# GpSimd's share of a feed-forward moved to VectorE, and one plain group in place of two, in a two-layer decoder trunk

## The chip, the cores and the metric

One core of one Trainium2 chip runs the whole program in one launch. The metric is the device time of one execution in microseconds; where several runs stand, the median is used. The engines are called as in the profile: PE (TensorE), PEld (its weight loads), DVE (VectorE), ACT (ScalarE), POOL (GpSimd), SP (the queue that issues the DMAs).

## The reference

The input is x, 1024 tokens of 1024 features in float32. Each of two layers does this (cut to what matters; d_ff is 2816):

```
h = rmsnorm(x);  proj = h @ w_in          # four token mixers read proj
y_a, y_b, y_c, y_d = latent attention, gated convolution, causal pooling, window attention
x = x + rmsnorm_per_group(y_a, y_b, y_c, y_d) @ w_o
h2 = rmsnorm(x)
gate, up = split(h2 @ w_gate_up)
x = x + (silu(gate) * up) @ w_down
```

A last rmsnorm follows. The change touches the feed-forward (the last three lines) and its neighbourhood.

## The kernel before

**Layout and exactness.** Features lie on the 128 partitions, tokens along the columns, in two token halves of 512 (`HT`). A float32 operand is split into two fp32r parts, hi and lo: ScalarE copies hi (L283, or L286 with a gain), VectorE makes lo as the difference (L284, L287). A product of two operands is then three TensorE instructions per 128-deep block, hi*hi, hi*lo and lo*hi (`mm3`, L272), each 128x128 by 128x512.

**The feed-forward by block products.** The activations are seen as a 2x2 matrix of blocks: even and odd feature tiles by the two token halves (B11, B21 of the one half, B12, B22 of the other; `hb` holds four tiles of each). The weights w_gate_up are handled in 22 groups `f` of 128 columns of d_ff; class `GateUp` loads a group's 2 x 512 KB (L1126). There are two ways to do a group:

- *plain*: `plain(f, u)` makes, for token half u, the gate from two block products and the up from two more, in PSUM banks taken from the rotation "wide". Both halves together make eight block products of four blocks each. `plain_gates`, `plain_silus`, `plain_acts` finish them.
- *seven products* (a Strassen-like form, the main loop over f from `NPL` to 21): it needs sums of weight blocks (`sums`, L1132 to L1134, and `sum4`, L1154, all on GpSimd) and sums of activation blocks N1, N2, T3, T4, which `combine(j)` makes on VectorE from both halves of feature tiles 2j and 2j+1. `gu_start` makes the first two products, on B11 and B21 only; the partial sums k1, k2, k5 are copied out of PSUM by ScalarE (`snap`, L1176) and added on VectorE (L1188, L1502, L1514).

`silu(g, r)` is ScalarE's Silu (L1311) followed by a product on GpSimd (L1312). `second` and `neg_mul` (L1305) make the activations. `combos(g)` (L1321, L1323) makes the sums of activation blocks that w_down's seven products need and writes them to DRAM. The sums of w_down's blocks are made meanwhile by the generator `dn_sums` (L157 to L164): per chunk a DMA in, four GpSimd sums of 128x256 (L161), a DMA out; 22 chunks a layer. The main loop steps it on with `next(sums, None)`.

With `NPL = 2` groups 0 and 1 are plain, so that TensorE has products to make as soon as one token half's residual is done (`out_last`, L1099), while VectorE still makes the other half's and the combinations.

**Storage.** 47 places of 4 KB per partition (`Slots`) serve weights and activations; PSUM has eight banks in four tags, mm (2), s (3), t (2), pv (1). `ps(tag)` takes the next bank of a tag, or of a rotation in `turns`.

**Order of the work.** The program order above is only a proposal. `order_engines` reads all instructions (`steps_of`), and `arrange` plays them through with a length for each (`length`) and writes the order of each engine's queue. Its rank is the program's own number plus a shift from the table `MOVES`, found by a search. Each engine then takes its queue strictly in that order. All of this runs on the host ahead of the launch.

Of the kernel before, what the change touches and what calls it, by code (L numbers as in the profile page):

```python
# [41 lines left out]
NPL = 2  # L42
# [69 lines left out]
def trunk_kernel(ctx: ExitStack, tc: tile.TileContext, ins, out):  # L112
# [37 lines left out]
    def dn_sums(l):  # L150

        n = HT // 2
        for c in range(0, NK // 2 * NG * P, n):
            cols = slice(c, c + n)
            i = F.pair()
            v = F.ap2(i).rearrange("p (b n) -> p b n", b=4)
            sp.dma_start(v, ins["w_dn"][l, :, :, cols].rearrange("b p n -> p b n"))  # L157
            yield
            b11, b12, b21, b22 = (v[:, k] for k in range(4))
            for k, (o, u) in enumerate(((b22, b21), (b21, b11), (b11, b22), (b12, b11))):  # L160
                pool.tensor_tensor(out=o, in0=o, in1=u, op=ALU.add)  # L161
# [225 lines left out]
    for l in range(L):  # L387
# [731 lines left out]
        class GateUp:  # L1119
# [8 lines left out]
            def sums(self):  # L1128
                w1, w2 = self.raw
                q = self.q = F.pair()  # L1130
                a11, a22, a21 = F.ap(w1), F.ap(w1 + 1), F.ap(w2 + 1)
                pool.tensor_tensor(out=F.ap(q + 1), in0=a21, in1=a22, op=ALU.add)  # L1132
                pool.tensor_tensor(out=F.ap(q), in0=a21, in1=a11, op=ALU.add)
                pool.tensor_tensor(out=a21, in0=F.ap(q + 1), in1=a11, op=ALU.add)  # L1134
# [17 lines left out]
            def sum4(self):  # L1152
                q4 = F.ap(self.raw[1])
                pool.tensor_tensor(out=q4, in0=q4, in1=F.ap(self.raw[1] + 1), op=ALU.add)  # L1154
# [24 lines left out]
        def gu_start(w, between=None):  # L1179

            w.pa, pd = ps("aa"), ps("ad")
# [5 lines left out]
            w.gate = tmp("tp")  # L1187
# [56 lines left out]
        for n in range(2):  # L1244
            R.free(kb_[1][n][1])
            R.free(va[2 + n][1])
        ma1 = norm_a(1)
        mix_values(*prev)
        for n in range(2):
            R.free(kb_[1][n][0])  # L1250
            R.free(va[n][1])
        ma0 = norm_a(0)
        out_some(len(parts))
# [3 lines left out]
        std = [GateUp(f) for f in range(2)]  # L1257
        std[0].split_plain()
# [4 lines left out]
        std[1].split_plain()  # L1263
# [4 lines left out]
        def plain(f, u):  # L1268

            w, b = std[f], ((B11, B21), (B12, B22))[u]  # L1270
            pg, pu = ps("wide"), ps("wide")
# [37 lines left out]
        def silu(g, r):  # L1309
            nonlocal last_silu  # L1310
            last_silu = act.activation(g, g, AF.Silu)  # L1311
            pool.tensor_tensor(out=g, in0=g, in1=r, op=ALU.mult)  # L1312
# [113 lines left out]
        w = GateUp(2)  # L1426
        plain(0, 0)
        combine(0)
        plain(1, 0)
        norm(0)  # L1430
        combine(1)
        plain_gates()
        plain(0, 1)
        norm(1)
        plain_silus()
        plain_gates()
        w.sums()
        combine(2)
        plain_acts()
        w.split1()  # L1440
        plain(1, 1)
        plain_silus()
        plain_gates()
        combine(3)
        w.split2()
        plain_acts()
# [3 lines left out]
        wn = GateUp(3)  # L1450
        w.split3()
        plain_silus()
        w.sum4()
        w.split4()
        plain_acts()
        for f in range(NPL, NFF):
            if wn:
                wn.sums()
            wnn = GateUp(f + 2) if f + 2 < NFF else None
            end = f == NFF - 1  # L1460
            gu_start(w, lambda: pending and second(*pending))
# [11 lines left out]
            if wn:  # L1473
# [5 lines left out]
            for i in w.s2:  # L1479
                R.free_pair(i)  # L1480
            k2 = snap(w.pa)
            if wn:
# [37 lines left out]
            neg_mul(F.ap(acts[f][0]), w.pa, gate)  # L1520
            if wn:
# [137 lines left out]
class Step:  # L1659
    __slots__ = ("ins", "eng", "rank", "before", "after", "tiles", "left", "ns", "tail", "ready", "sums", "bank", "onchip", "size", "start", "end", "table", "rows", "place")  # L1660

    def __init__(self, eng, rank):
# [4 lines left out]
        self.onchip = 0.0  # L1667
# [40 lines left out]
def length(eng, kind, i, ins, outs):  # L1708
    n = max(width(a) for a in ins + outs)
    ps = any(a.bass_ap.tensor.name.startswith("ps_") for a in ins)  # L1710
    if eng == "POOL":
        return 206 if kind == "InstMemset" else 1150 + 0.5 * n
# [19 lines left out]
def steps_of(tc):  # L1732
    steps, seen = [], {}
    table, runs = None, {"Silu": [], "Exp": []}
    for i in tc.nc.cur_bb.bb.instructions:
# [31 lines left out]
        else:  # L1767
            v.ns = length(eng, kind, i, ins, outs)
            if not any(a.bass_ap.tensor.name.startswith("ps_") for a in ins + outs):
                v.onchip = 0.7 if kind == "InstTensorScalarPtr" and len(ins) < 3 else 0.4  # L1770
# [39 lines left out]
def arrange(steps, rank=lambda v: v.rank):  # L1810
    queue, uses, freed, parked = {}, {}, {}, {}
# [21 lines left out]
    wire, pool_busy, last_fp32, table = 0.0, [], False, "Exp"  # L1833
# [5 lines left out]
    def takes(v, t):  # L1839
        for name in (x for x in v.tiles if x not in live):  # L1840
            tag = name.rsplit("_", 1)[0]
            if queue[tag][0] != name or not freed[tag] or freed[tag][0] + 40 > t:
# [3 lines left out]
    while any(now.values()) or any(later.values()):  # L1846
# [23 lines left out]
        for name in (x for x in v.tiles if x not in live):  # L1870
            tag = name.rsplit("_", 1)[0]
            if queue[tag][0] != name or not freed[tag]:
# [9 lines left out]
        for name in [x for x in v.tiles if x not in live]:  # L1882
            tag = name.rsplit("_", 1)[0]
            live.add(name)
            queue[tag].popleft()
            heapq.heappop(freed[tag])
# [17 lines left out]
        else:  # L1904
# [5 lines left out]
            if e == "DVE" and v.onchip:  # L1910
                ns += v.onchip * sum(max(0.0, min(b, t + ns) - max(a, t)) for a, b in pool_busy[-8:])
# [5 lines left out]
            if e == "POOL":  # L1917
                pool_busy.append((t, v.end))
# [6 lines left out]
        for name in v.tiles:  # L1925
            todo[name] -= 1
# [221 lines left out]
```

## Time and profile before

| | us |
|---|---|
| median of 3 runs | 2062.74 |
| lowest, highest | 2061.73, 2062.99 |
| the profiled execution, its own time | 2061.72 |
| its span, first to last instruction | 2059.9 |
| first layer: mixers, feed-forward entry, body, w_down | 0 to 380, to 520, to 840, to 1030 (about) |
| second layer: the same | 1030 to 1380, to 1520, to 1840, to 2060 (about) |

Some 1.8 us of the profiled execution lie outside the span. TensorE's granted clock is 0.998 of full speed over the span. Apart from small memsets GpSimd is at work from about 360 to 840 and from about 1400 to 1870 us. A row of the groups view reads: line, engine, operation, output and inputs with shapes, count | busy us, mean ns | idle time before it and what ended it. A row of the timeline reads: start, duration, engine, line, operation, count, and in brackets the idle time before it with what ended it. Matmul rows overlap (a row of 0.39 us starts every 0.23 us), so the busy share of PE is read as "no gap".

### The profile page before, as it was taken

The numbers are of one execution on the slowest core, as the hardware profiler recorded it, in microseconds if no ns is written. First come the engines' busy times: TensorE is split into PE (matmuls) and PEld (weight loads), VectorE is DVE, ScalarE is ACT, GpSimd is POOL, SyncE is SP. The second block draws the span as 40 slices with busy tenths as digits, with TensorE's granted clock in tenths as the row PEclk, the third lists the DMA queues.
The fourth block names the chain that finished last, engine by engine and source line by source line (L and its number), as shares of the span: only waits on it lengthen the run. The fifth ranks groups of instructions, "written<-read, shape, count | busy, mean of one in ns | idle before, by whom it ended". The sixth has DMA issues, their size and how long they took to land.

```text
span 2059.9 us, 26292 instructions
## 1 busy us (share of the span) xinstructions
PE 2033.0 (99%) x9418; PEld 1676.4 (81%) x9418; DVE 1553.8 (75%) x2430; ACT 979.5 (48%) x1722; POOL 596.9 (29%) x461
## 2 busy tenths in 40 slices
PE   8999999999999999999999999999999999999997
PEld 7887888878888888888888878878778888888887
DVE  7879988987776768655657898879877677686555
ACT  7447666653333334444443576666433333355332
POOL 0000000058776765100000000001787677640000
PEclk9999999999999999999999999999999999999999
DMA  5010222334444437866401102142444444498652
GB/s 181 34 58 24 79 88 86 138 121 168 170 156 167 166 138 257 313 221 204 152 33 44 47 21 91 64 144 81 160 168 163 153 166 153 145 333 278 197 177 86
DMA packets 148819, 289.76 MB, mean 141 GB/s; under 512 B 12608, under 2 KB 72000, under 8 KB 148688
## 3 DMA queue, kind: packets, MB, share of 16 engines
q1 hardware_dynamic: 148656, 288.03, 40.2%
q8 instruction: 74, 1.21, 0.2%
q14 instruction: 57, 0.47, 0.1%
q0 software_dynamic: 32, 0.04, 0.0%
HBM read 204.66 MB, written 83.36 MB: 140 GB/s over the span
## 4 chain that ended last, share of the span: by engine, by line
PE 89%; DVE 7%; DMA 1%; issue 1%; ACT 1%; POOL 1%; SPq 0%; DVEq 0%; ACTq 0%
PE ps_mm L272 35%; PE ps_s L272 26%; PE ps_t L272 10%; PE ps_pv L272 8%; DVE u L284 2%; PE ps_pv L962 2%; PE ps_t L950 1%; DVE u L287 1%; PE ps_s L896 1%; DVE u L324 1%; PE ps_t L336 1%; PE ps_s L898 1%; PE ps_s L897 1%; PE ps_pv L572 1%; DVE u L1099 1%
## 5 line engine op out<-in xcount | busy, mean ns | idle before, releaser
L272 PE MATMUL ps_mm<-u,u 128*128 128x512 f32 (+1 forms) x3394 | 848.8, 388 | 9.9 <-ACT u L286 7.1
L272 PEld LDWEIGHTS ps_mm<-u,u 128*128 128x128 f32 x3394 | 622.8, 188 | 136.2 <-ACT u L286 7.1
L272 PE MATMUL ps_s<-u,u 128*128 128x512 f32 x2648 | 649.4, 390 | 4.7 <-DVE u L284 3.6
L272 PEld LDWEIGHTS ps_s<-u,u 128*128 128x128 f32 x2648 | 496.8, 188 | 110.1 <-DVE u L284 4.4
L284 DVE TENSOR_TENSOR u<-u,u 128x1024 fp32r<-128x1024 f32 (+2 forms) x384 | 463.9, 1230 | 148.8 <-ACT u L283 129.3
L283 ACT CAST u<-u 128x1024 fp32r<-128x1024 f32 (+2 forms) x384 | 332.9, 888 | 464.9 <-PE ps_mm L272 178.4
L272 PE MATMUL ps_t<-u,u 128*128 128x512 f32 (+1 forms) x1146 | 274.4, 378 | 0.4 <-ACT u L283 0.4
L959 POOL MEMSET u<- 128x128 f32 x32 | 6.6, 230 | 847.8 <-PE ps_mm L272 637.8
L272 PEld LDWEIGHTS ps_t<-u,u 128*128 128x128 f32 x1146 | 206.3, 188 | 41.3 <-ACT u L283 0.8
L161 POOL TENSOR_TENSOR u<-u 128x256 f32<-128x256 f32 x176 | 196.8, 1118 | 73.2 <-DMA u<-in_w_dn 62.3
L1312 POOL TENSOR_TENSOR tp<-tp,u 128x512 f32<-128x512 f32 x88 | 147.1, 1672 | 209.6 <-ACT tp L1311 209.5
L272 PE MATMUL ps_pv<-u,u 128*128 128x512 f32 x744 | 184.7, 389 | 0.0
L272 PEld LDWEIGHTS ps_pv<-u,u 128*128 128x128 f32 x744 | 139.7, 188 | 29.0
L1311 ACT ACTIVATE tp<-tp 128x512 f32<-128x512 f32 x88 | 55.6, 632 | 134.1 <-DVE tp L348 133.4
L1132 POOL TENSOR_TENSOR u<-u,u 128x512 f32<-128x512 f32 x40 | 70.6, 1765 | 128.7 <-PE ps_s L272 55.5
L283 ACT CAST u<-ps_t 128x512 fp32r<-128x512 f32 (+4 forms) x136 | 64.8, 506 | 63.2 <-PE ps_t L950 38.9
L286 ACT ACTIVATE u<-u,par 128x512 fp32r<-128x512 f32 x100 | 69.3, 717 | 53.6 <-DVE u L1099 19.5
L284 DVE TENSOR_TENSOR u<-ps_t,u 128x512 fp32r<-128x512 f32 (+4 forms) x136 | 76.5, 583 | 17.8 <-ACT u L283 16.7
L287 DVE SCALAR_TENSOR_TENSOR u<-u,par,u 128x512 fp32r<-128x512 f32 x100 | 73.5, 757 | 7.5 <-ACT u L286 7.2
L348 DVE TENSOR_TENSOR tp<-tp,u 128x512 f32<-128x512 f32 x80 | 74.9, 936 | 1.1
L1514 DVE TENSOR_TENSOR tp<-ps_mm,tn 128x512 f32<-128x512 f32 x40 | 27.6, 690 | 63.4 <-PE ps_mm L272 63.4
L1154 POOL TENSOR_TENSOR u<-u 128x512 f32<-128x512 f32 x40 | 70.0, 1751 | 4.6 <-DVE u L284 4.6
(190 smaller groups left out, 2212.2 us busy)
## 6 DMA issues: line engine op xcount, KB each, us to landing
u<-in_w_gu SPq DMA_DIRECT2D x88, 512.0 KB, 4.3
ad<-u SPq DMA_DIRECT2D x154, 256.0 KB, 2.4
u<-ad SPq DMA_DIRECT2D x70, 512.0 KB, 5.8
u<-in_w_dn SPq DMA_DIRECT2D x68, 512.0 KB, 3.7
qd<-u SPq DMA_DIRECT2D x44, 512.0 KB, 2.9
u<-qd SPq DMA_DIRECT2D x32, 512.0 KB, 4.9
u<-in_w_in SPq DMA_DIRECT2D x30, 512.0 KB, 3.5
u<-in_xT SPq DMA_DIRECT2D x32, 256.0 KB, 5.0
```

The lines of the kernel that those rows point to most:

```text
L161: pool.tensor_tensor(out=o, in0=o, in1=u, op=ALU.add)
L272: pe.matmul(o, w, r, start=start and k == 0 and i == 0, stop=stop and k == n - 1 and i == 2, skip_group_check=again,)
L283: act.copy(hi, f)
L284: dve.tensor_tensor(out=lo, in0=f, in1=rd(hi), op=ALU.subtract)
L286: act.activation(hi, f, AF.Copy, scale=gain)
L287: dve.scalar_tensor_tensor(out=lo, in0=f, scalar=gain, in1=rd(hi), op0=ALU.mult, op1=ALU.subtract)
L348: dve.tensor_tensor(out=o, in0=a, in1=b, op=ALU.mult)
L962: pe.matmul(py[:, c0:], v_of(j, h), R.ap(s)[:, c0:], start=j == 0 and n == 0, stop=j == nj - 1 and n == 1,)
L1132: pool.tensor_tensor(out=F.ap(q + 1), in0=a21, in1=a22, op=ALU.add)
L1154: pool.tensor_tensor(out=q4, in0=q4, in1=F.ap(self.raw[1] + 1), op=ALU.add)
L1311: last_silu = act.activation(g, g, AF.Silu)
L1312: pool.tensor_tensor(out=g, in0=g, in1=r, op=ALU.mult)
```

## The change

Five parts, in the words of the diff:

1. The sums of w_down's blocks, the sums of w_gate_up's blocks and the product in `silu` are issued on `dve` instead of `pool`.
2. `NPL = 1`: only group 0 is plain; groups 1 to 21 take seven products.
3. The entry is rewritten. Group 0 is loaded ahead of `norm_a(1)` and split behind it; group 1 is loaded, summed and split around the last `mix_values` and `norm_a(0)`; group 2 is loaded behind `out_last` of the first half. The first two products of groups 1 and 2 are made early (`gu_start(..., early=True)`), in a bank of tag s, with the gate held in a place of its own (`w.place`) until the group ends. `plain` takes its banks from mm, mm for one half and t, s for the other.
4. The planner changes: GpSimd's length is 177 + 2.18 n ns instead of 1150 + 0.5 n; VectorE and GpSimd exclude each other for on-chip operands, where a part of the overlap was added before; a bank tag is held until the first user of a tile, by program order, has been placed.
5. `MOVES` is a new table.

```diff
-NPL = 2
+NPL = 1
...
-                pool.tensor_tensor(out=o, in0=o, in1=u, op=ALU.add)
+                dve.tensor_tensor(out=o, in0=o, in1=u, op=ALU.add)
...
-                pool.tensor_tensor(out=F.ap(q + 1), in0=a21, in1=a22, op=ALU.add)
-                pool.tensor_tensor(out=F.ap(q), in0=a21, in1=a11, op=ALU.add)
-                pool.tensor_tensor(out=a21, in0=F.ap(q + 1), in1=a11, op=ALU.add)
+                dve.tensor_tensor(out=F.ap(q + 1), in0=a21, in1=a22, op=ALU.add)
+                dve.tensor_tensor(out=F.ap(q), in0=a21, in1=a11, op=ALU.add)
+                dve.tensor_tensor(out=a21, in0=F.ap(q + 1), in1=a11, op=ALU.add)
...
-                pool.tensor_tensor(out=q4, in0=q4, in1=F.ap(self.raw[1] + 1), op=ALU.add)
+                dve.tensor_tensor(out=q4, in0=q4, in1=F.ap(self.raw[1] + 1), op=ALU.add)
...
-        def gu_start(w, between=None):
-            w.pa, pd = ps("aa"), ps("ad")
+        def gu_start(w, between=None, early=False):
+            w.pa, pd = ps("s" if early else "aa"), ps("ad")
...
-            w.gate = tmp("tp")
+            w.place = F.half() if early else None
+            w.gate = F.ap(w.place) if early else tmp("tp")
...
+        std = [GateUp(0)]
         ma1 = norm_a(1)
+        std[0].split_plain()
+        w = GateUp(1)
+        w.sums()
         mix_values(*prev)
...
+        w.split1()
         ma0 = norm_a(0)
+        w.split2()
         out_some(len(parts))
         out_last(HALVES[0], ma1)
...
-        std = [GateUp(f) for f in range(2)]
-        std[0].split_plain()
+        wn = GateUp(2)
         out_last(HALVES[1], ma0)
...
-        std[1].split_plain()
...
-            pg, pu = ps("wide"), ps("wide")
+            pg, pu = (ps("mm"), ps("mm")) if u == 0 else (ps("t"), ps("s"))
...
-            pool.tensor_tensor(out=g, in0=g, in1=r, op=ALU.mult)
+            dve.tensor_tensor(out=g, in0=g, in1=r, op=ALU.mult)
...
-        w = GateUp(2)
         plain(0, 0)
         combine(0)
-        plain(1, 0)
         norm(0)
+        gu_start(w, early=True)
         combine(1)
         plain_gates()
+        plain_silus()
+        plain_acts()
+        norm(1)
         plain(0, 1)
...
+        wn.sums()
+        wn.split1()
+        combine(2)
+        wn.split2()
+        gu_start(wn, early=True)
+        combine(3)
         w.split3()
...
-        return 206 if kind == "InstMemset" else 1150 + 0.5 * n
+        return 206 if kind == "InstMemset" else 177 + 2.18 * n
...
-                ns += v.onchip * sum(max(0.0, min(b, t + ns) - max(a, t)) for a, b in pool_busy[-8:])
+            if e in held and v.onchip:
+                ns += max(0.0, held["POOL" if e == "DVE" else "DVE"] - 138 - t)
+                held[e] = t + ns
```

More of the change, by code (lines that the diff above doesn't have):

```diff
@@ L1424, in norm @@
             r2.append(F.ap(ss2.rnorm(HALVES[u], tag="pv", parts=True)))
-        w = GateUp(2)
         plain(0, 0)
         combine(0)
-        plain(1, 0)
         norm(0)
+        gu_start(w, early=True)
         combine(1)
         plain_gates()
+        plain_silus()
+        plain_acts()
+        norm(1)
         plain(0, 1)
[L1434 to L1446, printed above, removed]
         for hl in hb[B12]:
@@ L1449, in trunk_kernel @@
                 R.free(i)
-        wn = GateUp(3)
+        wn.sums()
[4 more added lines that the diff above has]
+        combine(3)
         w.split3()
-        plain_silus()
+        plain_gates()
         w.sum4()
         w.split4()
+        plain_silus()
         plain_acts()
         for f in range(NPL, NFF):
-            if wn:
+            soon = f == NPL
+            if wn and not soon:
                 wn.sums()
-            wnn = GateUp(f + 2) if f + 2 < NFF else None
+            wnn = GateUp(f + 2) if f + 2 < NFF and not soon else None
             end = f == NFF - 1
-            gu_start(w, lambda: pending and second(*pending))
+            if f > NPL + 1:
+                gu_start(w, lambda: pending and second(*pending))
+            elif pending:
+                second(*pending)
             for g in [*range(NPL // 2 if f == NPL else 0), *range(f // 2, f // 2 + f % 2)]:
@@ L1472, in trunk_kernel @@
             mul_to(gate, gate, r2[0])
-            if wn:
+            if wn and not soon:
                 wn.split1()
@@ L1480, in trunk_kernel @@
                 R.free_pair(i)
+            if soon:
+                wnn = GateUp(f + 2)
             k2 = snap(w.pa)
-            if wn:
+            if wn and not soon:
                 wn.split2()
@@ L1520, in trunk_kernel @@
             neg_mul(F.ap(acts[f][0]), w.pa, gate)
+            if w.place is not None:
+                F.free(w.place)
             if wn:
@@ L1666, in __init__ @@
         self.sums = self.bank = None
-        self.onchip = 0.0
+        self.onchip = False
         self.table = self.rows = None
@@ L1769, in steps_of @@
             if not any(a.bass_ap.tensor.name.startswith("ps_") for a in ins + outs):
-                v.onchip = 0.7 if kind == "InstTensorScalarPtr" and len(ins) < 3 else 0.4
+                v.onchip = kind != "InstMemset"
             if ins:
@@ L1810, in arrange @@
 def arrange(steps, rank=lambda v: v.rank):
-    queue, uses, freed, parked = {}, {}, {}, {}
+    queue, uses, freed, parked, held_by = {}, {}, {}, {}, {}
     for v in steps:
@@ L1832, in arrange @@
     out = {e: [] for e in SIGNAL}
-    wire, pool_busy, last_fp32, table = 0.0, [], False, "Exp"
+    wire, last_fp32, table = 0.0, False, "Exp"
+    held = {"DVE": 0.0, "POOL": 0.0}
     before = {e: ((0, 0), 0.0) for e in SHIFT}
@@ L1841, in takes @@
             tag = name.rsplit("_", 1)[0]
-            if queue[tag][0] != name or not freed[tag] or freed[tag][0] + 40 > t:
+            if queue[tag][0] != name or tag in held_by or not freed[tag] or freed[tag][0] + 40 > t:
                 return False
@@ L1871, in arrange @@
             tag = name.rsplit("_", 1)[0]
-            if queue[tag][0] != name or not freed[tag]:
+            if queue[tag][0] != name or tag in held_by or not freed[tag]:
                 parked[tag].append((k, n, v))
@@ L1885, in arrange @@
             queue[tag].popleft()
+            if uses[name][0] is not v:
+                held_by[tag] = uses[name][0]
             heapq.heappop(freed[tag])
@@ L1909, in arrange @@
                     t = max(t, end + SHIFT[e])
-            if e == "DVE" and v.onchip:
-                ns += v.onchip * sum(max(0.0, min(b, t + ns) - max(a, t)) for a, b in pool_busy[-8:])
+            if e in held and v.onchip:
+                ns += max(0.0, held["POOL" if e == "DVE" else "DVE"] - 138 - t)
+                held[e] = t + ns
             if v.table and v.table != table:
@@ L1916, in arrange @@
             free[e] = v.end - OVERLAP[e]
-            if e == "POOL":
-                pool_busy.append((t, v.end))
             if v.tail:
@@ L1925, in arrange @@
         for name in v.tiles:
+            tag = name.rsplit("_", 1)[0]
+            if held_by.get(tag) is v:
+                del held_by[tag]
+                for x in parked[tag]:
+                    heapq.heappush(later[x[2].eng], (v.start + 1, *x))
+                parked[tag] = []
             todo[name] -= 1
```

112 rows, old and new, of the table MOVES are left out of this document.

## The prediction

> **What bounds the kernel now.** I read the head of the page first, then the busy time by stages, then TensorE's own waits.
>
> ```profile
> span 2059.9 us, 26292 instructions
> ...
> PE 2033.0 (99%) x9418; PEld 1676.4 (81%) x9418; DVE 1553.8 (75%) x2430; ACT 979.5 (48%) x1722; POOL 596.9 (29%) x461
> ```
>
> TensorE is busy for 2033.0 of 2059.9 us, so only fewer products, or fewer waits of TensorE, can shorten the run. The stages say where waits are (columns: window, then busy us and count of PE, PEld, DVE, ACT, POOL, then clock, DMA share, GB/s):
>
> ```profile
> 550.00:800.00 250.00, 250.00 (x1105) 207.07 (x1104) 175.57 (x174) 86.94 (x120) 174.41 (x128) 1.00 0.47 164
> ...
> 380.00:520.00 140.00, 137.19 (x603) 112.52 (x602) 123.05 (x146) 69.16 (x105) 74.39 (x52) 1.00 0.40 138
> 1380.00:1520.00 140.00, 136.72 (x597) 111.03 (x596) 126.25 (x151) 74.73 (x113) 69.90 (x46) 1.00 0.39 137
> ```
>
> 550 to 800 is the body of the first layer's feed-forward: TensorE has no gap, 1105 products in 250 us, 0.2262 us each. The two windows below are the two feed-forward entries: TensorE lacks 2.8 and 3.3 us there, and VectorE is busy for 123 and 126 of 140 us. What TensorE waited for in the whole run (total us, times, longest):
>
> ```profile
> PE ps_mm L272 <- ACT u L286: 7.1, 1, 7.1
> PE ps_s L272 <- DVE u L284: 3.6, 2, 2.4
> PE ps_mm L272 <- ACT u L215: 1.9, 2, 1.0
> PE ps_s L336 <- DVE u L320: 1.4, 1, 1.4
> PE ps_s L272 <- DVE te L1502: 1.1, 1, 1.1
> PE ps_mm L272 <- DVE u L284: 0.9, 1, 0.9
> ```
>
> The 7.1 is the program's first load. The waits on L284 and L1502 are in the entries: 3.6 + 1.1 + 0.9 = 5.6 us, all on VectorE. L215 and L320 (3.3 us) are in other stages.
>
> **The change part by part.**
>
> **One plain group fewer.** A plain group makes 4 products in each token half, each over 4 blocks of hb with 3 TensorE instructions a block: 2 x 4 x 12 = 96. A group of the main loop makes seven (B11, B21, N2, N1, T3, B22, T4): 84. Group 1 of each layer goes from 96 to 84, so 24 instructions go in the two layers: 24 x 0.2262 = **5.43 us**. Nothing covers this: TensorE is the bound, and the weight loads go with the products.
>
> **GpSimd's work on VectorE.** By the code it is 2 x 22 x 4 = 176 sums of 128x256 (L161), 88 products in `silu` (L1312), and in each main-loop group three sums and a fourth (L1132 to L1134, L1154), now 42 groups where 40 were: 256 operations of 128x512 in all. What they cost on VectorE is read from other operations of the same shapes there, and what they cost GpSimd from the body of the feed-forward:
>
> ```profile
> L348 DVE TENSOR_TENSOR u<-u,u 128x512 f32<-128x512 f32 x39 | 25.6, 685 | 0.2
> ...
> L284 DVE TENSOR_TENSOR u<-vraw,u 128x256 fp32r<-128x256 f32 x2 | 0.8, 408 | 0.0
> ...
> 380.52 1.27 DVE L1099 TENSOR_TENSOR u<-u,ps_s 128x512 f32<-128x512 f32 x2
> ```
>
> ```profile
> L161 POOL TENSOR_TENSOR u<-u 128x256 f32<-128x256 f32 x52 | 55.1, 1059 | 10.7 <-DMA u<-in_w_dn 6.2 <-DVE u L1305 1.3
> L1312 POOL TENSOR_TENSOR tp<-tp,u 128x512 f32<-128x512 f32 x27 | 45.5, 1684 | 42.6 <-ACT tp L1311 42.6
> L1154 POOL TENSOR_TENSOR u<-u 128x512 f32<-128x512 f32 x13 | 22.7, 1744 | 0.0
> L1132 POOL TENSOR_TENSOR u<-u,u 128x512 f32<-128x512 f32 x12 | 21.4, 1782 | 21.8 <-PE ps_s L272 21.8
> L1133 POOL TENSOR_TENSOR u<-u,u 128x512 f32<-128x512 f32 x12 | 15.9, 1327 | 0.0
> L1134 POOL TENSOR_TENSOR u<-u,u 128x512 f32<-128x512 f32 x12 | 15.5, 1294 | 0.9
> ```
>
> An operation of 512 columns takes 0.685 us, and two back to back 1.27 us, so the second adds 0.60: neighbours overlap by about 0.08. In the 250 us of the body, 76 such operations add 76 x 0.60 = 45.6 us, and 52 short ones at 0.408 - 0.08 = 0.33 add 17.2: 62.8 us.
>
> Against that stands what GpSimd takes from VectorE today. The same forms in the body, and without GpSimd's work (from 850 to 1050, and for L1050 on tiles of the entry):
>
> ```profile
> L284 DVE TENSOR_TENSOR u<-u,u 128x1024 fp32r<-128x1024 f32 x40 | 66.5, 1688 | 11.1 <-ACT u L283 10.5
> L348 DVE TENSOR_TENSOR tp<-tp,u 128x512 f32<-128x512 f32 x27 | 22.7, 840 | 0.4
> L1050 DVE SCALAR_TENSOR_TENSOR u<-u,u 128x512 f32<-128x512 f32 x14 | 16.1, 1150 | 0.2
> L1305 DVE SCALAR_TENSOR_TENSOR u<-te,tp 128x512 f32<-128x512 f32 x13 | 15.3, 1179 | 7.1 <-POOL tp L1312 7.1
> ...
> L284 DVE TENSOR_TENSOR u<-u,u 128x1024 fp32r<-128x1024 f32 x42 | 50.7, 1223 | 31.6 <-ACT u L283 28.8 <-PE ps_pv L272 1.9 <-PE ps_mm L272 0.7
> ...
> L1050 DVE SCALAR_TENSOR_TENSOR tp<-tp,te 128x512 f32<-128x512 f32 x8 | 6.1, 759 | 0.1
> ```
>
> 40 x 465 ns + 27 x 155 + 14 x 391 + 13 x 420 = 33.8 us come back. VectorE goes from 175.6 to 175.6 - 33.8 + 62.8 = 204.6 of 250 us: 82%. TensorE is full there and stays full, so I cost the body at **0**. The cover is the double buffers: a group of 84 products is 19 us, its weights are split a group ahead, and its `pd` and `pc` banks are two deep. If that cover went, each late VectorE operation would show in full, 0.60 us a group.
>
> **The entries.** Scaling the body's net (62.8 - 33.8 = 29.0 us for 174.4 us of GpSimd work, 0.166) to 74.4 and 69.9 us of GpSimd work adds 12.4 and 11.6: VectorE would stand at 135 and 138 of 140. That is full. Two things move in opposite directions. First, GpSimd no longer makes VectorE late where TensorE waits for it:
>
> ```profile
> 448.81 1.76 POOL L1134 TENSOR_TENSOR u<-u,u 128x512 f32<-128x512 f32 x1
> ...
> 449.36 1.76 DVE L348 TENSOR_TENSOR tp<-tp,u 128x512 f32<-128x512 f32 x1
> ...
> 451.05 1.21 DVE L284 TENSOR_TENSOR u<-u,u 128x1024 fp32r<-128x1024 f32 x1
> ...
> 452.31 0.50 PE L272 MATMUL ps_s<-u,u 128*128 128x512 f32 x1 [2.41 <-DVE u L284]
> ```
>
> ```profile
> 1450.45 1.30 POOL L1312 TENSOR_TENSOR tp<-tp,u 128x512 f32<-128x512 f32 x1 [7.17 <-ACT tp L1311]
> ...
> 1450.52 2.31 DVE L284 TENSOR_TENSOR u<-u,u 128x1024 fp32r<-128x1024 f32 x1 [0.23 <-PE ps_s L272]
> ...
> 1455.72 2.56 PE L272 MATMUL ps_mm<-u,u 128*128 128x512 f32 x10 [0.92 <-DVE u L284]
> ```
>
> At 449.36 an operation of 0.685 us lasts 1.76, to 0.55 us after GpSimd's sum ends, and the split behind it is what TensorE waits for: 1.08 us of that wait are GpSimd's. In the second layer the split at 1450.52 takes 2.31 for 1.22, more than the 0.92 that TensorE then waits. I take **2.0 us** for the two; the other 3.6 us of the entries' waits I leave. The Trainium skill ("SBUF — State Buffer", Who interferes with whom) has the same pair exclude each other for a whole instruction, but only where VectorE reads two SBUF inputs; by that the relief ends with these forms, and the sum stays.
>
> Second, TensorE gets there sooner. Before, 192 plain products (two groups) stood between the residual's last products and those that need the combinations of `combine`. Now it is plain group 0 (96) and the two early starts (24 each), 144; 48 fewer are 10.9 us less cover per layer. The combinations must come that much earlier from VectorE, which has the sums of groups 1 and 2 besides. It has room ahead: the loads and first splits of groups 0 and 1 now stand around the last values and `norm_a(0)`, where it is not full:
>
> ```profile
> 360.00:370.00 10.00, 10.00 (x45) 8.03 (x44) 6.35 (x9) 6.52 (x9) 3.84 (x3) 1.00 0.76 280
> ...
> 1360.00:1370.00 10.00, 10.00 (x51) 7.94 (x51) 5.74 (x11) 5.54 (x10) 0.41 (x2) 1.00 0.19 68
> ```
>
> New waits here are bounded by 0 and 10.9 us a layer. The estimate of 135 to 138 of 140 is just under full, so I take the near end, 0.5 us a layer: **+1.0**. New waits by banks are in this too: `plain(0, 1)` now takes a `t` bank, which an early start's `pd` holds until VectorE's sum L1188 has read it, and behind a late L1188 stand the splits.
>
> **Loads, queues, order.** Weight loads of groups 0 to 2 move ahead on the SP queue; the DMA share in the entry windows is 0.40, so they land in time: 0. If not, the split waits, and its ScalarE queue with it. The order search renumbers everything. Outside the entries TensorE's waits sum to 3.3 us beside the first load, so it can win 3.3; it could lose as much. I take 0.
>
> **Sum.** The profiled execution took 2061.72 us (its span 2059.9 and 1.8 around it). 2061.72 - 5.43 - 2.0 + 1.0 = 2055.29. The median of the runs, 2062.74, is 1.02 above it: **2056.3**.
>
> **The rivals.**
>
> **Entries without waits**: the order search finds places for all of it and the 5.6 us go entirely: 2062.74 - 5.43 - 5.6 = 2051.7. For it speaks that VectorE's operations get one fixed length, so that a planned order holds; against it, that VectorE is full there.
>
> **Saving eaten**: some 5 us of new waits in the entries, 2.5 a layer: about 2061 with the two GpSimd waits gone as above. For it: 144 products of cover for a full VectorE.
>
> **Entries run dry, slower**: VectorE delivers the last combinations as late as now, and TensorE waits for the whole missing cover, 10.9 us a layer: 2062.74 - 5.43 + 21.8 = 2079. It decides from 4.8 us a layer on (9.6 less 5.43 is over 4.1). Against it: the DVE rows above get shorter in just these windows. The Trainium skill ("Perfetto Trace Analysis", Optimizing Scalar/DVE Operations) advises to take work off a full VectorE, to GpSimd too, though it doubts a gain between these two; the trace's 391 to 465 ns per operation side with the doubt. "TensorE: Matmul & The Clock Gate" (Part 1) in the Trainium skill halves the clock after some 3.4 us of idling, which would lengthen such a wait; the longest wait here, 2.41 us, left the granted clock at 1.00.
>
> **VectorE late in the body**: if the rows' excess is not GpSimd's doing, VectorE stands at 175.6 + 62.8 = 238 of 250 us, and waiting in order it would be late by an operation in each group: 42 x 0.60 = 25 us, 2082. Against it: the excess is missing where GpSimd rests (1223 against 1688).
>
> **How the numbers follow.** Forecast 2056.3 (2053.5 to 2059.5): 0.57. Entries without waits, 2051.7: 0.15. Saving eaten, 2061: 0.14. Entries dry, 2079: 0.11. Body late: 0.03. The range reaches from the second case with part of the 3.3 us elsewhere, 2049.5, to the third with a bit more, 2064. A measurement of this kernel can tell 0.2%, 4.1 us, from no change. Faster is below 2058.6: most of the forecast (0.50) and the second case, 0.65. Same: the rest of the forecast, the third case: 0.21. Slower: 0.14.
>
> **What would show it.** Right: 24 TensorE instructions fewer; GpSimd left with its memsets; L284 of 128x1024 at 1.22 us everywhere; the body at 0.226 us a product with VectorE near 82%; entry windows lacking 2 to 5 us together. Wrong: TensorE rows with waits on VectorE above 3 us before the first N2 or N1 products, or any gap in the body.

## The result, and the profile after

The changed kernel takes 2056.95 us (median of 8 runs, 2055.43 to 2058.7), beside 2062.86 us (8 runs, 2061.43 to 2063.55) for the kernel before on the same chips: ratio 0.9972, 95% interval 0.9962 to 0.9982, or 5.9 us less by the medians. The forecast was 2056.3. Its terms did not come out one by one, though, and the experiments say which.

The head of the page of the kernel after:

```profile
span 2055.1 us, 26087 instructions
...
PE 2031.7 (99%) x9394; PEld 1669.6 (81%) x9394; DVE 1616.3 (79%) x2872; ACT 991.3 (48%) x1738; POOL 6.7 (0%) x37
```

TensorE has 9394 instructions where it had 9418, the 24 of the forecast; GpSimd is left with its memsets, and VectorE took its work for 62.5 us more busy time in the whole run. The windows view of the same kernel, columns as before:

```profile
380.00:520.00 140.00, 139.15 (x609) 113.37 (x608) 127.94 (x204) 73.58 (x111) 0.00 (x0) 1.00 0.41 142
550.00:800.00 250.00, 250.00 (x1104) 206.99 (x1104) 201.16 (x306) 89.19 (x122) 0.00 (x0) 1.00 0.49 169
1380.00:1520.00 140.00, 138.62 (x604) 112.26 (x603) 129.62 (x205) 78.47 (x120) 0.00 (x0) 1.00 0.43 151
```

The body is as full as it was. The entries hold 609 and 604 products in 140 us, where 603 and 597 stood. What TensorE waits for now, by the waits view of after (total us, times, longest):

```profile
PE ps_mm L272 <- ACT u L286: 7.2, 1, 7.2
PE ps_s L336 <- DVE u L320: 1.4, 1, 1.4
PE ps_mm L272 <- DVE u L829: 1.1, 3, 0.5
PE ps_mm L272 <- DVE u L1099: 1.1, 2, 0.6
PE ps_mm L272 <- ACT u L215: 0.8, 1, 0.8
PE ps_mm L272 <- ACT u L283: 0.8, 1, 0.8
```

The waits on L284 and L1502 (5.6 us before) are gone. New are short ones on L1099, the residual, and L283, a split. In the timeline each entry has one of either kind, the first at its beginning and the second before the combined blocks:

```profile
397.62 1.65 PE L272 MATMUL ps_mm<-u,u 128*128 128x512 f32 x6 [0.48 <-DVE u L1099]
424.44 0.50 PE L272 MATMUL ps_s<-u,u 128*128 128x512 f32 x1 [0.37 <-ACT u L283]
...
1392.82 1.67 PE L272 MATMUL ps_mm<-u,u 128*128 128x512 f32 x6 [0.62 <-DVE u L1099]
1443.13 0.73 PE L272 MATMUL ps_mm<-u,u 128*128 128x512 f32 x2 [0.76 <-ACT u L283]
```

The groups by form in the body of the first layer, 550 to 800, show VectorE's operations without GpSimd beside them:

```profile
L284 DVE TENSOR_TENSOR u<-u,u 128x1024 fp32r<-128x1024 f32 x41 | 49.8, 1219 | 4.7 <-ACT u L283 4.6
L161 DVE TENSOR_TENSOR u<-u 128x256 f32<-128x256 f32 x52 | 22.0, 422 | 1.8 <-DMA u<-in_w_dn 1.1
L1317 DVE TENSOR_TENSOR tp<-tp,u 128x512 f32<-128x512 f32 x27 | 18.6, 689 | 6.3 <-ACT tp L1316 6.3
L348 DVE TENSOR_TENSOR tp<-tp,u 128x512 f32<-128x512 f32 x26 | 17.9, 690 | 0.6
L1050 DVE SCALAR_TENSOR_TENSOR u<-u,u 128x512 f32<-128x512 f32 x14 | 9.6, 685 | 0.0
```

The same forms took 1688 (L284), 840 (L348) and 1150 ns (L1050) before. L161 and the product in `silu`, now L1317, are new on VectorE at 422 and 689 ns, for the 408 and 685 that were assumed.

One thing I had not looked for is in the groups of ScalarE, whole run, of after and of before's program with its engine moved (e1, below):

```profile
L1316 ACT ACT_TABLE_LOAD x4 | 5.1, 1283 | 0.2
L338 ACT ACT_TABLE_LOAD x2 | 2.6, 1283 | 0.0
L339 ACT ACT_TABLE_LOAD x2 | 2.6, 1283 | 0.0
```

```profile
L1311 ACT ACT_TABLE_LOAD x2 | 2.6, 1283 | 0.0
```

These lines are Silu and the two functions of `norm` (Ln and Exp). In after, `norm(1)` stands behind the first `plain_silus()`, so ScalarE changes its function table four times in each entry, where both kernels with two plain groups change it once: 3 x 1.283 = 3.85 us more on ScalarE. In the first entry all four loads (413.32 to 423.24) stand ahead of the wait on L283 that is quoted above, in the second three of them (1430.49, 1433.38 and 1435.80), the last at 1449.92 behind it:

```profile
421.96 1.28 ACT L1316 ACT_TABLE_LOAD   x1
423.25 0.63 ACT L1316 ACTIVATE u<-u 128x512 f32<-128x512 f32 x1
423.79 0.60 ACT L283 CAST u<-tp 128x512 fp32r<-128x512 f32 x1
...
1433.38 1.28 ACT L338 ACT_TABLE_LOAD   x1
1434.67 0.60 ACT L338 ACTIVATE tn<-ps_pv 128x512 f32<-128x512 f32 x1
1435.17 0.61 ACT L283 CAST u<-tp 128x512 fp32r<-128x512 f32 x1
1435.80 1.28 ACT L339 ACT_TABLE_LOAD   x1
...
1442.04 1.04 ACT L283 CAST u<-u 128x1024 fp32r<-128x1024 f32 x1
```

Waits leave out short delays. So I also summed, over the whole trace, the time from the start of one product to the start of the next beyond the usual pitch of its width (227 ns for 512 columns, 175, 120 and 109 for 384, 256 and 128; a step shorter than the pitch counts against it). This is TensorE's lost time, in us, by stage:

| stage | before | after | e1 | e5 | e11 |
|---|---|---|---|---|---|
| 0 to 350 | 14.7 | 16.2 | 14.9 | 15.6 | 16.7 |
| 350 to 550, first entry | 3.9 | 2.8 | 1.3 | 2.7 | 10.0 |
| 1050 to 1350 | 10.7 | 12.0 | 11.4 | 11.3 | 11.2 |
| 1350 to 1550, second entry | 6.8 | 4.7 | 1.9 | 4.3 | 11.7 |
| 550 to 1050 and 1550 to the end | 1.0 | 1.7 | 1.1 | 1.4 | 1.5 |
| sum | 37.2 | 37.4 | 30.5 | 35.3 | 51 |

After and e5 share all but 24 instructions in each layer's group 9, so their other stages show how far one profile differs from the next: some 0.7 us a stage. The table says the odd thing of this case: the changed kernel loses as much as before, 37.4 for 37.2, and gains just the products it leaves out.

### The profile page after: what moved, and what is told of

Same layout as the page of the kernel before. It is cut to its first block, busy times and chain, and to the rows that moved or that the text cites. A ratio compares the mean times of both kernels' runs of the same rounds, so it can differ in the third digit from the quotient of the medians.

```text
span 2055.1 us, 26087 instructions
## 1 busy us (share of the span) xinstructions
PE 2031.7 (99%) x9394; PEld 1669.6 (81%) x9394; DVE 1616.3 (79%) x2872; ACT 991.3 (48%) x1738; POOL 6.7 (0%) x37
## 4 chain that ended last, share of the span: by engine, by line
PE 92%; DVE 3%; ACT 2%; DMA 1%; issue 1%; SPq 0%; DVEq 0%; ACTq 0%
PE ps_mm L272 36%; PE ps_s L272 29%; PE ps_t L272 11%; PE ps_pv L272 8%; PE ps_pv L962 1%; PE ps_t L950 1%; PE ps_s L896 1%; PE ps_t L336 1%; PE ps_pv L572 1%; PE ps_s L898 1%; PE ps_s L897 1%; DMA u<-in_w_o 1%; PE ps_s L511 1%; PE ps_mm L770 1%; DVE u L324 1%
## 5 line engine op out<-in xcount | busy, mean ns | idle before, releaser
L283 ACT CAST u<-u 128x1024 fp32r<-128x1024 f32 (+2 forms) x388 | 335.9, 889 | 392.6 <-PE ps_s L272 85.6
L284 DVE TENSOR_TENSOR u<-u,u 128x1024 fp32r<-128x1024 f32 (+2 forms) x388 | 389.4, 1020 | 148.2 <-ACT u L283 122.4
L272 PE MATMUL ps_t<-u,u 128*128 128x512 f32 (+1 forms) x1118 | 265.3, 378 | 0.0
L272 PE MATMUL ps_pv<-u,u 128*128 128x512 f32 x696 | 172.0, 390 | 0.0
L272 PEld LDWEIGHTS ps_pv<-u,u 128*128 128x128 f32 x696 | 130.3, 188 | 27.9 <-ACT tn L1176 0.6
L283 ACT CAST u<-ps_t 128x512 fp32r<-128x512 f32 (+4 forms) x136 | 64.8, 506 | 73.7 <-PE ps_t L560 35.6
L284 DVE TENSOR_TENSOR u<-ps_t,u 128x512 fp32r<-128x512 f32 (+4 forms) x136 | 76.2, 582 | 14.1 <-ACT u L283 13.6
L1176 ACT COPY tn<-ps_s 128x512 f32<-128x512 f32 x66 | 38.4, 582 | 90.0 <-PE ps_s L272 89.2
L161 DVE TENSOR_TENSOR u<-u 128x256 f32<-128x256 f32 x176 | 73.8, 421 | 3.7 <-DMA u<-in_w_dn 1.7
L318 ACT ACTIVATE tn<-u 128x512 f32<-128x512 f32 (+1 forms) x93 | 53.1, 590 | 35.3 <-DVE u L1575 31.8
L216 DVE TENSOR_TENSOR u<-u,u 128x1024 fp32r<-128x1024 f32 (+1 forms) x46 | 51.9, 1129 | 22.4 <-ACT u L215 12.7
L1317 DVE TENSOR_TENSOR tp<-tp,u 128x512 f32<-128x512 f32 x84 | 57.6, 688 | 13.0 <-ACT tp L1316 12.2
L348 DVE TENSOR_TENSOR tp<-tp,u 128x512 f32<-128x512 f32 x80 | 54.8, 688 | 1.3
L215 ACT CAST u<-u 128x1024 fp32r<-128x1024 f32 (+1 forms) x46 | 44.7, 973 | 20.3 <-DMA u<-in_w_in 16.9
```

The source lines that it names most:

```text
L161: dve.tensor_tensor(out=o, in0=o, in1=u, op=ALU.add)
L215: act.copy(hi[:, :n], raw[:, :n])
L216: dve.tensor_tensor(out=lo[:, :n], in0=raw[:, :n], in1=rd(hi[:, :n]), op=ALU.subtract)
L272: pe.matmul(o, w, r, start=start and k == 0 and i == 0, stop=stop and k == n - 1 and i == 2, skip_group_check=again,)
L283: act.copy(hi, f)
L284: dve.tensor_tensor(out=lo, in0=f, in1=rd(hi), op=ALU.subtract)
```

## The experiments

The operations added in e6 to e8, e11 and e12 write an idle tile, `more`, that nothing reads; e5 makes one product twice. In e1, e2, e5 to e8, e11 and e12 every instruction keeps the shift that `MOVES` gave it, added ones have none; the bookkeeping for this is left out of the diffs below. The planner still lays the queues out anew from the changed lengths.

**e1: the kernel before with the engine moved, and nothing else.** All of the sums and products on GpSimd go to VectorE; two plain groups, the old entry and the old `MOVES` stay.

```diff
-                pool.tensor_tensor(out=o, in0=o, in1=u, op=ALU.add)
+                dve.tensor_tensor(out=o, in0=o, in1=u, op=ALU.add)
...
-            pool.tensor_tensor(out=g, in0=g, in1=r, op=ALU.mult)
+            dve.tensor_tensor(out=g, in0=g, in1=r, op=ALU.mult)
```

> The kernel before with only the engine move: GpSimd's sums and products go to VectorE, two plain groups stay, and the shifts of the order table stay with the same instructions. Theory A (the gain is 24 products fewer, the engine move takes only waits behind GpSimd out of the entries): no products go, so about 2 us below before, 2061, ratio 0.999; TensorE keeps 9418 instructions. Rival B (the engine move is the gain, the products' saving is lost to the thinner cover): 5 us or more below before, ratio 0.997 or less. Rival C (the order search is the gain): the old shifts do not fit the new lengths, 2065 or more.

Measured: 2055.46 us beside 2061.69, ratio 0.9968 (0.9955 to 0.9980): 6.2 us, as much as the whole change. Windows and waits of e1:

```profile
380.00:520.00 140.00, 140.00 (x616) 114.80 (x615) 129.58 (x202) 71.59 (x108) 0.00 (x0) 1.00 0.41 143
550.00:800.00 250.00, 250.00 (x1104) 207.01 (x1104) 199.12 (x302) 88.70 (x121) 0.00 (x0) 1.00 0.48 165
1380.00:1520.00 140.00, 140.00 (x616) 115.06 (x615) 130.90 (x202) 74.51 (x112) 0.00 (x0) 1.00 0.40 136
```

```profile
PE ps_mm L272 <- ACT u L286: 7.0, 1, 7.0
PE ps_s L336 <- DVE u L320: 1.4, 1, 1.4
PE ps_mm L272 <- ACT u L215: 1.3, 2, 1.1
PE ps_pv L572 <- ACT u L283: 0.4, 1, 0.4
PE ps_s L272 <- DVE te L1502: 0.4, 1, 0.4
```

Both entries run without a gap, 616 products in 140 us, with VectorE busy for 130. Against before that is (616 - 603) + (616 - 597) = 32 products, 32 x 0.2262 = 7.2 us. Of the 5.6 us of waits on VectorE there, 0.4 is left. The waits went with GpSimd's work, not only the two that the prediction counted. How GpSimd makes a wait from a distance is seen in the timeline of before, ahead of the wait on L1502 in its second entry:

```profile
1482.69 1.75 DVE L284 TENSOR_TENSOR u<-u,u 128x1024 fp32r<-128x1024 f32 x1
...
1484.97 1.93 DVE L284 TENSOR_TENSOR u<-u,u 128x1024 fp32r<-128x1024 f32 x1
1486.82 1.23 DVE L348 TENSOR_TENSOR tp<-tp,u 128x512 f32<-128x512 f32 x1
1487.97 0.68 DVE L1502 TENSOR_TENSOR te<-ps_s,tn 128x512 f32<-128x512 f32 x1
...
1488.70 1.65 PE L272 MATMUL ps_s<-u,u 128*128 128x512 f32 x6 [1.14 <-DVE te L1502]
```

VectorE has no idle time here. L1502, which TensorE waits for, reads PSUM and takes its usual 0.68 us. But three of the four operations ahead of it, those that read two operands on chip, take 0.53, 0.71 and 0.55 us more than their 1.22 and 0.685: 1.79 us for a wait of 1.14. Since e1 is also laid out anew, a part of its 6.2 us can be the order's; the run doesn't separate the two.

**e2: the changed kernel with the work back on GpSimd.** The reverse edit.

> The changed kernel with the engine move undone: the sums and products are on GpSimd again, one plain group, the new order table on the same instructions. Theory A: 24 products fewer stay, the waits behind GpSimd come back in the entries, 2 to 4 us above the changed kernel, 2059 to 2061, still below before. Rival B: the whole gain goes, 2062 or more. Rival C: the search was made for VectorE's lengths, so several us of new waits, 2065 or more.

Measured: 2079.08 us, ratio 1.0084 (1.0070 to 1.0098), some 1.1% or 23 us over the changed kernel. The entries' lost time is 12.9 and 15.3 us, where after has 2.8 and 4.7; that is 20.7 of it. TensorE's clock stood at 0.50 for 6.83 us in each entry, an estimated 4 to 5 us of this (some 23 products at 0.43 us for 0.23). So the new entry, in this order, stands only with VectorE free of GpSimd. The order was made for VectorE's lengths, which may be a part of this; the direction agrees with e1, the size isn't the engine's alone.

**e3 and e4: both kernels without their order search**, `MOVES = {}`.

> The kernel before with an empty order table, so the planner's rank is the program's own number. This gives the worth of the search before. All theories: slower than before, by 5 to 40 us. To be read with the same for the changed kernel.

> The changed kernel with an empty order table. Theory A: as far below the unsearched kernel before as the changed kernel is below before, 5 to 6 us, or some more, since VectorE's lengths are no longer disturbed. Rival B: 5 us or more below, with all of it in TensorE's waits. Rival C: no faster than the unsearched kernel before.

Measured: before becomes 2087.82 (1.0126, 1.0112 to 1.0140), after 2079.21 (1.0084, 1.0070 to 1.0098). The tables are worth some 26 us to the one and 23 to the other; unsearched, the change brings 8.6 us for 5.9. So the gain doesn't need the new search: the program has it without a table. The planner's new rules (part 4) are in e4 but not in e1, which has the gain too, so it doesn't need them either.

**e5: the products put back.** 24 TensorE instructions more in the changed kernel, in the body, where all else is hidden.

```diff
+            if between and f == 9:
+                product(pd, blocks(w.s2, 0), hb[B21], extra=True)
             product(pd, blocks(w.s2, 0), hb[B21])
```

> The changed kernel with 24 products put back in the body: in group 9 of each layer the 12 instructions of the product on B21 are made twice, the second time over the first. It prices the products alone. Theory A: 24 x 0.2262 = 5.4 us above the changed kernel, 2062.4, which is the time of before. Rival B (a part of a product's time is cover for other waits): less than 3 us above.

Measured: 2062.07 us, ratio 0.9993 (0.9984 to 1.0003), by the ratios 4.3 us over the changed kernel, by the medians 5.1; its page has TensorE at 9418 instructions and 2036.7 us busy, 5.0 more. The price of 5.43 us lies within the interval, which is some 2 us wide to either side.

**e6, e7, e8: more work for VectorE, misplaced.** Five (e6) or nine (e7) operations of 128x384 in each main-loop group from 4 on, or six ahead of `combine(2)` in each layer (e8), each reading a constant:

```diff
+            if f > 3 and not end:
+                for _ in range(5):
+                    dve.tensor_tensor(out=more, in0=more, in1=cst[:, 0 : 3 * P], op=ALU.max)
```

> The changed kernel with five idle VectorE operations of 128x384 (0.47 us each back to back) added in each group from 4 to 20, 2.4 us in 19: VectorE goes from 80% to about 92% of the body. Theory A (the body's cover holds while VectorE is below full): no change, within 1 us of the changed kernel. Rival D (VectorE late in the body): 17 groups x 2 layers x 0.5 us or more, 17 us up.

> The same with nine such operations, 4.2 us in 19: by the sum VectorE would need 102% of the body. Both theories: slower, and the step from five to nine shows where the cover ends. Theory A: 34 x 0.5 us of excess, about 10 to 20 us up, from the body alone. Rival D: 50 us or more.

> The changed kernel with six such VectorE operations (2.8 us) added once in each layer, at the entry just ahead of the third call of combine. It asks whether VectorE is full at the entry. If it is, as forecast, TensorE waits for 2 to 2.8 us more in each layer: 4 to 6 us up, 2061 to 2063. If it has room left, within 1 us of the changed kernel.

Measured: 2081.04 (1.0083, 1.0068 to 1.0097), 2080.8 (1.0086, 1.0073 to 1.0099) and 2057.0 (0.9969, 0.9958 to 0.9981). None of them put its work where it was meant to stand, as the tile view of e6 shows (durations min, median, max; first and last start):

```profile
L1523 DVE TENSOR_TENSOR more<-more,cst x170: 534/553/561, 25.6 to 564.5; 128x384 f32<-128x384 f32 x170
```

Nothing held the operations, so the planner issued them where VectorE seemed free: all 170 within the first 565 us, mostly in the first layer's mixers, and e8's twelve in the first 47 us. 94 us more on VectorE there (170 x 0.553) cost 24 us, 20.7 of them between 350 and 550 by the measure of the table above, and twelve operations at the very start cost nothing. e7 has as many operations before 500 us as e6, and most of the rest in the body: there VectorE is busy for 247.4 of 250 us between 550 and 800, and TensorE lacks 0.4. So nine a group cost no more than five. e11 and e12 repeat the test with operations tied to their place.

**e9, e10: planned with slack.** To tell whether the changed kernel's short waits come from an order planned too tightly or from the cover that it has lost, both programs (after, and e1's) were given a new table, searched with 8 ns more for each VectorE and ScalarE operation. The expectations' theory E is the order, theory F the cover.

```diff
-            v.ns = length(eng, kind, i, ins, outs)
+            v.ns = length(eng, kind, i, ins, outs) + (8 if eng != "POOL" else 0)
```

> The changed kernel, same program, with an order table searched anew for it, from lengths with 8 ns more for every VectorE and ScalarE operation, so that the order leaves some slack. Open since the engine move alone gave the whole gain: why the 24 products fewer gained nothing on top. Theory E (the order is at fault: it was placed with no slack, and slips in the entries and mixers): the 6.8 us of lost TensorE time that the changed kernel has over the engine move alone mostly go, 2050 to 2052. Theory F (the thinner cover is at fault, 144 products in place of 192 ahead of the combinations): they stay, 2055 to 2057, with TensorE's gaps in the entries.

> The engine move alone (two plain groups), with an order table searched anew in the same way and for as long, so that both programs have had the same. Its entries have no gap to take away. Theory E and F: 2054 to 2056, no change from the engine move alone. Should it come as far down as the changed kernel does with its new table, the 24 products would be worth nothing; theory E puts it 5 us above that one, theory F level with it.

Measured: 2080.27 (1.0082, 1.0069 to 1.0094) and 2092.08 (1.0136, 1.0121 to 1.0152). Both missed. In the windows of e10 TensorE has gaps even where it never had one, in the body (below) and in w_down, where it is busy for 187.5 of 190 us:

```profile
550.00:800.00 250.00, 249.35 (x1088) 201.68 (x1087) 191.45 (x299) 84.29 (x117) 0.00 (x0) 1.00 0.47 160
```

Outside mixers and entries, e9 lost 19.3 and e10 27.6 us, where after lost 1.7. The new tables are worse in the entries too, and far worse behind them, so they decide nothing between E and F.

**e11: 2.8 us of VectorE in each entry, tied.** Six operations of 128x384 ahead of `combine(2)`, reading a residual tile that is ready only there.

```diff
+        for _ in range(6):
+            dve.tensor_tensor(out=more, in0=more, in1=F.ap(x[4][0])[:, 0 : 3 * P], op=ALU.max)
         combine(2)
```

> Six idle VectorE operations of 128x384 (2.8 us) in each entry, as before, but each reads the residual tile of feature tile 4, so that they cannot run at the program's start, where the last ones went. If VectorE is full at the entry, 4 to 6 us up, 2061 to 2063; if there is room, within 1 us of the changed kernel, 2057.

Measured: 2068.84 us, ratio 1.0027 (1.0017 to 1.0038), 11.9 us over the changed kernel by the medians, 11.3 by the ratios: some 6 us a layer for 2.8 us of work. Windows of e11:

```profile
380.00:520.00 140.00, 135.02 (x579) 107.92 (x578) 125.28 (x199) 72.99 (x110) 0.00 (x0) 0.99 0.39 132
1380.00:1520.00 140.00, 135.50 (x577) 108.41 (x576) 129.66 (x207) 77.66 (x120) 0.00 (x0) 0.98 0.43 146
...
1450.00:1455.00 5.00, 2.43 (x10) 1.63 (x8) 5.00 (x9) 4.39 (x7) 0.00 (x0) 0.89 0.00 0
1455.00:1460.00 5.00, 5.00 (x13) 3.43 (x12) 4.91 (x8) 1.87 (x4) 0.00 (x0) 0.50 0.48 124
1460.00:1465.00 5.00, 5.00 (x22) 4.07 (x21) 3.96 (x8) 4.66 (x8) 0.00 (x0) 0.93 0.50 185
```

30 and 27 products fewer than after in the two windows. VectorE is busy for the whole 5 us in which TensorE stops in the second layer, though its 140 us window shows 130 with room left. The cost is over twice the work. A part is TensorE's clock: by the trace's clock records it stood at 0.50 for 6.83 us from 1453.90 in the second entry, and for 3.41 us from 429.90 in the first. Some 21 products fell in there, at 0.43 us for 0.23: an estimated 4 us. The rest, some 7 to 8 us, is more than the 5.6 us of added work; the planner lays the entry out anew around the six operations, so that isn't accounted for.

**e12: 3.3 us of VectorE in each body group, tied.** Seven operations reading `up`, in groups 4 to 20.

```diff
+            if f > 3 and not end:
+                for _ in range(7):
+                    dve.tensor_tensor(out=more, in0=more, in1=up[:, 0 : 3 * P], op=ALU.max)
```

> Seven idle VectorE operations of 128x384 (3.3 us) in each group from 4 to 20, each reading that group's up, so that they run in the body and not ahead of it: VectorE goes from 80% to about 97% there. Theory A (the body's cover holds while VectorE is below full): within 1 us of the changed kernel, 2057. Rival D: 17 us or more up.

Measured: 2056.18 us, ratio 0.9968 (0.9956 to 0.9981): no cost. The window of e12 that answers to the body's above, and the tile view that shows where its operations are:

```profile
550.00:800.00 250.00, 250.00 (x1103) 206.37 (x1102) 237.70 (x401) 86.40 (x121) 0.00 (x0) 1.00 0.49 166
```

```profile
L1523 DVE TENSOR_TENSOR more<-more,te x238: 544/551/560, 486.6 to 1811.3; 128x384 f32<-128x384 f32 x119
```

VectorE stands at 237.7 of 250 us, 95%, and TensorE has no gap. The added operations are planned work, which the planner places where it can; a VectorE that runs late against the plan is another matter, and wasn't tried.

## Why the prediction was right, and where it was not

**One plain group fewer, -5.43: right as a price.** 24 instructions fewer, and e5 gives them 4.3 to 5.1 us. But "nothing covers this" looked at TensorE alone. The plain products were work that TensorE could do while VectorE caught up; see the third step.

**GpSimd makes VectorE late, -2.0: right mechanism, mis-sized.** e1 gives 6.2 us for this, its new layout included. The prediction took the two waits where an operation beside GpSimd's ended just ahead of TensorE's wait, "the other 3.6 us of the entries' waits I leave". They went too, all but 0.4 us. VectorE takes its queue in order, so a delay by GpSimd is still there several operations later, when TensorE waits for one that GpSimd didn't touch (the rows at 1482.69 to 1488.70 above). Of the 2.41 us at 452.31 the prediction took the 1.08 of one operation. The rows of the body held what was needed: 33.8 us of excess in 250 us, and in the entries VectorE has little idle time to soak it up. (The "only" in the prediction's sentence on two SBUF inputs is more than these runs show; the slowed rows shown here all read two operands on chip.) The rival "entries without waits" is what e1 shows, with the plain group still in place.

**Less cover, +1.0: right sign, mis-sized.** The entries of after hold (616 - 609) + (616 - 604) = 19 products fewer than those of e1, 19 x 0.2262 = 4.3 us; the table of lost time gives the same, (2.8 - 1.3) + (4.7 - 1.9) = 4.3. That is the place and the size of "saving eaten", 1.5 and 2.8 us a layer for the 2.5 that it named. e11 shows how steep it is: the new entry has no room for 2.8 us more on VectorE. What makes these 4.3 us isn't settled. Three things could: the thinner cover itself, the order found for it, and the three table loads more on ScalarE, 3.85 us a layer around the beginning of the combined blocks, which the prediction overlooked. The single waits point to more than one cause. The two on L283 (0.37 and 0.76 us) stand behind table loads. The two on L1099 (0.48 and 0.62 us) end 16 and 38 us ahead of the first load of their entry (413.32 and 1430.49), before any combination is needed, so neither the loads nor the cover ahead of the combinations makes them. e9 and e10 failed to tell the first two apart; the six operations of e11 in an entry with two plain groups, and the changed kernel with `norm(1)` ahead of the first `plain_silus()`, were not tried. The second is the version that I would run next, and it can't touch the waits on L1099.

**Body, 0: right, with more room than I saw.** VectorE takes 201.2 us for a forecast of 204.6, L284 1219 ns for 1.22 us, TensorE has no gap. Even 95% is free there (e12), so the fourth rival's ground, "late by an operation in each group" at 238 of 250 us, was wrong: nearly full isn't late. That it is the double buffers that carry this was argued and not tested.

**Entries' VectorE at 135 to 138 of 140: too high, but full all the same.** It measured 128 to 131. The scaling from the body was the error: by it GpSimd took 33.8 x 74.4 / 174.4 = 14.4 us from VectorE in the first entry and 13.5 in the second. Against the median of the same forms in e1, the operations in the two windows of before took 23.0 and 22.9 us more. VectorE waits for inputs in the rest; e11 shows that the share of a 140 us window hides stretches with no room.

**Loads and order, 0: nearly, outside the entries.** The mixers lose 1.9 us more in after than in e1 and the other stages 0.6, 2.5 together, near what two profiles differ by.

**The sum.** By the runs: engine -6.2, products -5.4, entries +4.3, the other stages +2.5: -4.8, which is what the two profiled spans differ by (2059.9 and 2055.1), for a measured -5.9 between the medians. The forecast had -2.0, -5.4, +1.0 and 0: -6.4. Its number was right by luck: it took too little for the engine and too little for the cover, and the two errors cancel. The signs that it named for being right all came true (24 instructions, L284 at 1.22 us, the body's pace, entries that lack 2.2 us together) and couldn't tell this. **The changed kernel doesn't beat e1**: 0.9972 and 0.9968, with intervals that overlap. So far as these runs can tell, the engine move is the gain, and the products that were saved are given back in waits. No version here beat both by more than the measurement can tell.

**Entries dry, slower** (2079) did not come: the longest new wait is 0.76 us. e2 comes out at that number, with GpSimd's work in the new entry.

## What to carry to other kernels

Price a clash of two engines through the in-order queue behind it: add the excess durations up over the stretch where the slowed engine is full, and do not count only the waits where the clash stands beside the waiter. Work that an engine does while another catches up is cover; before removing it, test how much room the other has at just that place, with a few tied operations (an operation with ready inputs goes elsewhere). And a share of busy time says little either way: 95% was free in the body, and at 91% in the first entry there was no room.

## What the hardware showed that was not expected

**A stop of about 2 us can halve TensorE's clock, and its length alone doesn't decide.** In the timeline of e11:

```profile
1454.35 1.22 PE L274 MATMUL ps_mm<-u,u 128*128 128x512 f32 x2 [2.57 <-ACT u L285]
```

From 1453.90 the granted clock is 0.50 for 6.83 us (the windows of e11 above show most of it). The first entry of e11 has a shorter stop, 2.15 us up to 429.68, and the clock falls there too:

```profile
425.00:430.00 5.00, 1.55 (x4) 0.80 (x5) 5.00 (x9) 4.51 (x8) 0.00 (x0) 0.99 0.01 3
430.00:435.00 5.00, 5.00 (x15) 3.32 (x15) 5.00 (x9) 1.73 (x4) 0.00 (x0) 0.67 0.32 107
```

In e2 the slice 1490 to 1495 has 0.50 and 12 products, behind a stop of 1.90 us and 5 us with TensorE busy for 1.65. Before had a wait of 2.41 us, longer than two of these three, and its window shows the clock unharmed:

```profile
450.00:455.00 5.00, 2.69 (x12) 2.23 (x13) 5.00 (x5) 1.68 (x2) 3.71 (x3) 1.00 0.77 267
```

The clock records of all the traces show a pattern. Every stretch at 0.50, but for the one at a program's end, lasts 3.41 us or a whole multiple of it, and within a trace the stretches begin whole multiples of 3.41 us apart (e11: 429.90 and 1453.90, 300 times 3.413). So the clock seems to be set for 3.41 us at a time, by what TensorE did in the 3.41 us before, and a stop that falls across such an edge can pass. Ahead of 14 of the 15 falls in these traces TensorE was busy for 0.2 to 1.7 of the 3.41 us, ahead of the last for 2.2. Before's poorest stretch, 448.37 to 451.78 if its edges are counted back from the fall at the program's end, has 1.5 us and kept the clock. So the runs give no sharp limit. The Trainium skill ("TensorE: Matmul & The Clock Gate", Part 1) names an idle window of some 3.4 us. The length agrees; here a window needn't be idle throughout.

**A change of ScalarE's table costs 1.28 us here, and no drain shows.** The row before the load at 1433.38 ends at 1433.36 (1432.32 + 1.04); the load ends at 1434.66, and the function starts at 1434.67. The Trainium skill ("ScalarE: Activation LUTs", What ACT_TABLE_LOAD costs) adds some 1.38 us of drain to the 1.283 of the load; the trace has the load's figure and nothing behind it.
